# Four RMSNorm factors from two products of ones with the split sum of squares, instead of column factors, a GpSimd root and diagonals

## The chip, the cores and the metric

One core of a Trainium2 chip runs the whole program. The metric is the device time of one execution in microseconds; the kernel before took 1065.73 us, the median of three runs (1065.53 to 1066.01). The core's engines are TensorE (PE in the profile, its weight loads PEld), VectorE (DVE), ScalarE (ACT), GpSimd (POOL) and SyncE (SP), which issues nearly all of the transfers.

## The reference

A trunk of four layers over one sequence of 256 tokens with 1024 channels, all in float32. Each layer adds a token mixer and then a squared-ReLU MLP; each of these begins with an RMSNorm:

```python
def _rmsnorm(x, g):
    return x * lax.rsqrt(jnp.mean(x * x, axis=-1, keepdims=True) + EPS) * g

def _sqrelu_mlp(h, w1, w2):                 # w1: 1024 x 4096, w2: 4096 x 1024
    return jnp.square(jax.nn.relu(h @ w1)) @ w2

for i in range(4):                          # mixers: LRU, SGU, short conv, LRU
    x = x + mixer[i % 3](_rmsnorm(x, norm_mix_g[i]))
    x = x + _sqrelu_mlp(_rmsnorm(x, norm_mlp_g[i]), mlp_w1[i], mlp_w2[i])
return _rmsnorm(x, final_norm_g)
```

The LRU mixer multiplies the normed x by a 1024 x 2560 matrix; half of the result is a GELU branch, the other half goes through a causal convolution over 4 tokens, two gates with 16 blocks of 80 x 80 each, and a linear recurrence over the tokens. The short convolution's first matrix is 1024 x 3072.

## The kernel before

**Layout and numbers.** Channels lie on the 128 partitions and the 256 tokens along the free axis, so x is eight pieces of 128x256, held in pairs (x_105 to x_108). TensorE runs its large products in fp32r, a rounded form of float32, and keeps the accuracy by splitting each operand into a rounded part (hi) and the rest (lo): `mm3` (line 252) makes three products for each tile, hi by hi, hi by lo, lo by hi. Activations are split where they are made. Line 292 (ScalarE) and 293 (VectorE) make `xs`, the split x times the norm's gain; a norm's factor, one number for each token, is multiplied in only behind the first product.

**Weights.** SyncE streams them in chunks of 128x2048 into `raw` buffers. ScalarE rounds each half (line 186, `whi`) and VectorE subtracts (line 189, `wlo`), up to four chunks ahead of the product, into five pairs of buffers. These casts and splits are most of what both engines do.

**The norm's factor.** ScalarE squares x (line 303) and VectorE adds the eight pieces up (lines 308, 309) into `sum`, 128x256: what is left is the sum over the 128 partitions. There are two ways to finish.

`Scales` (six norms: the four mixers', and those of MLP 0 and 3):
- `first_mm` (line 331): two products, in plain float32, with `sum` as the stationary side and two columns of ones as the moving one. Tokens now lie on the partitions, two columns of 128. The trace has four records for these two products.
- `factor`: ScalarE copies 128x2 out of PSUM (line 314); GpSimd takes the reciprocal root by an integer seed (line 315) and three Newton steps (lines 318 to 321), and splits the result (lines 338, 339).
- `diagonals` (line 348): VectorE multiplies the identity by each of the four columns, 128x128 each.
- `second_mm` (line 361): two products of a matrix of ones by the diagonals, 128x256, which lay the factors out as a row on all partitions.
- `copy` (line 365): ScalarE takes that row, `rs`, out of PSUM. VectorE multiplies by it: line 486 in the MLP's hidden tiles, 744 and 824 in the LRU mixers.

`LateScale` (MLP 1 and 2) splits `sum` itself (lines 376, 377) and makes two products of ones by its halves (line 382), which gives the row of sums on all partitions at once; a reciprocal follows (lines 384, 385). The squared ReLU lets it do without the root, and its factor is wanted only behind the whole MLP.

The norm of the last layer's end works in another way; neither it nor the late ones change.

**Order.** TensorE's instructions stand as the program writes them; a helper, `in_mm(4, {k: f})`, runs over k = 0 to 7 (the eight pieces of x), four tiles of `mm3` for each k, and calls f behind step k. On VectorE and ScalarE a list scheduler sets the order by priority, and `SOON` (100) lifts a norm's steps. Two stretches are written out by hand: the first hidden tiles of an MLP by `MLP_STEPS` (C and S are a weight half's cast and split, h0 and h1 the next step of a pair of hidden tiles, `row` the copy of line 365), and each LRU mixer by a string in `LRU_STEPS`, in which P is one step of TensorE's list, `na nv nd nb nr` are `first_mm`, `factor`, `diagonals`, `second_mm` and `copy`, and for the pairs of tiles 0 to 4 `x` is the product with the row (line 744), `K` the convolution's first tap on ScalarE (line 752), `k` its other three taps on VectorE (line 758). Then come the gates (TensorE, lines 702, 710 and 717), their activations on ScalarE (line 770) and the recurrence. Line 803 loads the root's table on ScalarE, line 782 that of the exponential.

In an MLP, `first` (product, root and diagonals) stands behind k = 5 of the first block, `second_mm` behind k = 3 of the next. In the short convolution `first` stands behind k = 6 and `second` behind k = 3 of the following group.

Of the kernel before, what the change touches and what calls it, by code (L numbers as in the profile page):

```python
# [78 lines left out]
)  # L79


# [1 line left out]

HEAD_STEPS = "x0 w x1 w w x2 x3 q0 w w x4 x5 q1 w w x6 x7 q2 w q3"

MLP_STEPS = "C S row C h0 S h0 h0 h0 C h1 S h1 h1 h1 C S"

MLP_STEPS_LATE = "C S C h0 h0 h0 S h0 C h1 h1 h1 S h1 C S"

LATE_SPLIT, LATE_SUM = 3, 4  # L90

UNSPLIT = (0, 1)

# [17 lines left out]
def trunk(ctx: ExitStack, tc: tile.TileContext, xT, consts, sbias, first, weights, out, widths, whole, causal):  # L113
# [26 lines left out]
    def wtile(dtype=F32, name="wk"):  # L140
        return wide.tile([P, 2, T], dtype, name=name, tag="wk", bufs=N_WIDE)
# [182 lines left out]
    class Scales:  # L324
# [42 lines left out]
        def second(self):  # L367
            self.second_mm()
            self.copy()

    class LateScale:


# [17 lines left out]
    def in_mm(nm, hooks={}):  # L391

        banks = [bank() for _ in range((nm + 1) // 2)]
        parts = [(0, KD)] if nm == 2 else [(0, KD // 2), (KD // 2, KD)]
        for k0, k1 in parts:
            w_hi, w_lo = chunk(k1 - k0, nm * P)
            for k in range(k0, k1):
                for m in range(nm):
                    s = slice(m * P, (m + 1) * P)
                    o = banks[m // 2][:, (m % 2) * T:(m % 2 + 1) * T]  # L400
                    mm3(o, w_hi[:, k - k0, s], w_lo[:, k - k0, s], xs_now[k][0], xs_now[k][1],
                        start=k == 0 and m % 2 == 0, stop=k == KD - 1)
                if k in hooks:
                    hooks[k]()
        return [b.rearrange("p (j t) -> p j t", t=T) for b in banks]
# [68 lines left out]
    def mlp(nxt):  # L474


        late = nxt[0] is not None and nxt[1] > KD
        scale = LateScale() if late else Scales()

        def hidden_steps(ps, srcs):  # L480

            u, hi, lo, sq = wtile(name="u"), wtile(F32R, "hi"), wtile(F32R, "lo"), wtile(name="hsq")
            if late:
                yield nc.scalar.activation(u, ps, AF.Relu)  # L484
            else:
                yield nc.vector.scalar_tensor_tensor(out=u, in0=ps, scalar=0.0, in1=both(scale.row), op0=MAX, op1=MULT)  # L486
            yield nc.scalar.activation(hi, u, AF.Square)  # L487
            yield nc.scalar.activation(sq, u, AF.Square)  # L488
            srcs += tiles_of((hi, lo))
            yield nc.vector.tensor_tensor(out=lo, in0=sq, in1=hi.bitcast(F32), op=SUB)  # L490

        def hidden(banks):
            srcs = []
            for ps in banks:
                for _ in hidden_steps(ps, srcs):
                    pass
            return srcs

        def hidden_in_order(banks):

            srcs, pairs, in_order = [], {}, chain()
            for step in (MLP_STEPS_LATE if late else MLP_STEPS).split():
                if step in "CS":
                    in_order((casts if step == "C" else splits).pop(0)())
                elif step == "row":
                    in_order(scale.copy())
                else:
                    i = int(step[1:])
                    if i not in pairs:
                        pairs[i] = hidden_steps(banks[i], srcs)  # L510
                    in_order(next(pairs[i]))
            for steps in pairs.values():
                for _ in steps:
                    raise ValueError("steps of the hidden tiles are left")
            return srcs

        def second(acc, b, srcs):
            if b == NF - 1 and nxt[0] is None:

                x = x_res[KD // 2 - 1][:, 1, :]  # L520
                nc.vector.tensor_tensor(out=x, in0=acc[KD // 2 - 1][:, T:], in1=x, op=ADD)
                apart.append(bank())
                out_mm(acc, srcs, 4 * b, 4 * NF, apart[0])
            elif b == NF - 1:
                out_mm(acc, srcs, 4 * b, 4 * NF)
            else:
                for h in range(2):
                    out_mm(acc, srcs[2 * h:2 * h + 2], 4 * b + 2 * h, 4 * NF)

        apart = []  # L530
        placed[0] = True
        banks = in_mm(4, {} if late else {5: scale.first})
        acc = None
        for b in range(1, NF):
            hooks = {}
            if late and b == LATE_SPLIT:
                scale.split()
            if late and b == LATE_SUM:
                hooks = {3: scale.sum}
            if not late and b == 1:  # L540
                hooks = {3: scale.second_mm}
            nxt_banks = in_mm(4, hooks)
            if acc is None:
                before = hidden_in_order(banks)
                acc = [bank() for _ in range(KD // 2)]
                placed[0] = False
                with tc.high_priority(offset=-LATER):
                    make_parts()
            now = hidden(nxt_banks)
            second(acc, b - 1, before)  # L550
            before = now
        second(acc, NF - 1, before)
        if nxt[0] is None:
            return add_last(acc, apart[0])
        return add_residual(acc, *nxt, scale.row if late else None)
# [36 lines left out]
    class Mixer:  # L592


        def __init__(self, layer):
            self.layer = layer
            self.scale = Scales()
            self.banks = {"branch": [], "gated": [], "gates": {}}
            self.xr, self.xc, self.hs, self.gs, self.parts = {}, {}, {}, {}, {}
            self.rg, self.ig, self.qs, self.t = {}, {}, {}, {}  # L600
            self.acc = None
            self.in_order = chain()
            self.tensor = self.tensor_steps()
# [118 lines left out]
            return self.xc[m // 2][:, m % 2, :]  # L722


        def na(self):
            self.scale.first_mm()

        def nb(self):
            self.scale.second_mm()
# [86 lines left out]
        def z(self, i):  # L816
            self.hs[i] = h = self.rg[i]
            return [nc.vector.tensor_tensor_scan(out=h[:, j, :], data0=self.qs[i][:, j, :], data1=self.ig[i][:, j, :],
                                                 initial=0.0, op0=MULT, op1=ADD) for j in range(2)]


        def g(self, i):
            self.gs[i] = wtile(name="gate")
# [102 lines left out]


    def mixer_c(layer):
        scale = Scales()
        conv = []  # L930
        for b in range(2):
            gc = []
            g_banks = in_mm(4, {} if b else {6: scale.first})
            x_banks = in_mm(4, {} if b else {3: scale.second})
            for ps in g_banks:
                t = wtile(name="gc")
                nc.vector.tensor_tensor(out=t, in0=ps, in1=both(scale.row), op=MULT)
                gc.append(t)
            for i, ps in enumerate(x_banks):
                xv = wtile(name="xv")  # L940
                nc.vector.tensor_tensor(out=xv, in0=ps, in1=both(scale.row), op=MULT)
                nc.vector.tensor_tensor(out=xv, in0=xv, in1=gc[i], op=MULT)
                y = wtile(name="cv")
                for j in range(2):
                    m = 4 * b + 2 * i + j

                    def tap(n):
                        return col("c_conv_w", (layer * 3 + n) * KD + m)

                    nc.scalar.activation(y[:, j, :], xv[:, j, :], AF.Copy, scale=tap(2))  # L950
                    for n in (1, 0):
                        d = 2 - n
                        nc.vector.scalar_tensor_tensor(
                            out=y[:, j, d:], in0=xv[:, j, :T - d], scalar=tap(n), in1=y[:, j, d:],
                            op0=MULT, op1=ADD)
                conv.append(y)
        srcs = []
        for b in range(2):
            for i, ps in enumerate(in_mm(4)):
                y = conv[2 * b + i]  # L960
                gb = wtile(name="gb")
                nc.vector.tensor_tensor(out=gb, in0=ps, in1=both(scale.row), op=MULT)
                nc.vector.tensor_tensor(out=y, in0=y, in1=gb, op=MULT)
                srcs += tiles_of(split(y))
        return out_proj(srcs, 4)
# [230 lines left out]
```

## Time and profile before

| what | us |
|---|---|
| median of three runs | 1065.73 |
| the profiled execution's own time | 1065.78 |
| its span (first to last instruction) | 1064.1 |
| SP's main queue (q1), 201.75 MB | 55.7% of 16 DMA engines over the span |
| GpSimd, root's seed of line 315, 7 instructions | 12.9 |
| VectorE, diagonals of line 348, 24 instructions | 5.4 |

The granted clock of TensorE is 0.999 over the span. A row of the timeline gives the start in us, the busy time of a run of like instructions, engine, line, operation, tiles written and read, shape and how many; in square brackets stands the idle time ahead of it and what ended that. A grouped row gives the count, then the busy time and the mean ns of one, then the idle time ahead of them.

In this execution the norms' first products (line 331) start at 18.27 us in LRU layer 0, 111.26 in MLP 0, 531.75 in the short convolution, 792.50 in LRU layer 1 and 888.49 in MLP 3.

### The profile page before, as it was taken

To read this page: it belongs to the slowest core of one execution; us is meant where nothing else is said; L and a number is where in the kernel's file an instruction comes from. 1 tells how busy PE (TensorE), PEld (TensorE's weight loads), DVE (VectorE), ACT (ScalarE), POOL (GpSimd) and SP (SyncE) were. 2 spreads that over 40 slices of the span, in tenths; PEclk is the share of its full clock that TensorE was granted. 3 is DMA by queue.
4 is the path that set the end of the run, shared out by engine and by line. 5 is a ranking of instruction groups with operands and counts; after the bars stand their busy time and mean duration, and the time that the engine had idled before them with its cause. 6 is when DMAs were issued, how large, how long until landed. Compare 5 with 4: busy or idle time off the path is not lost.

```text
span 1064.1 us, 21687 instructions
## 1 busy us (share of the span) xinstructions
PE 1057.1 (99%) x9138; PEld 1044.4 (98%) x9138; DVE 712.6 (67%) x936; ACT 603.6 (57%) x851; POOL 48.4 (5%) x135
## 2 busy tenths in 40 slices
PE   9999999999999999999999999999999999999997
PEld 9999999999999999999999999999999999999997
DVE  7999765555758754545787765454578997755553
ACT  7697554454574754445544474455555975644442
POOL 2400100000210000000010000000010001000000
PEclk9999999999999999999999999999999999999999
DMA  9656575555556566555466466555545445855401
GB/s 341 252 234 218 173 282 190 195 193 190 190 177 216 178 210 207 188 194 178 157 235 200 159 221 204 193 189 184 194 154 177 179 145 184 294 197 194 138 1 40
DMA packets 58417, 203.39 MB, mean 191 GB/s; under 512 B 6608, under 2 KB 7760, under 8 KB 58320
## 3 DMA queue, kind: packets, MB, share of 16 engines
q1 hardware_dynamic: 58176, 201.75, 55.7%
q8 instruction: 71, 1.16, 0.4%
q14 instruction: 26, 0.21, 0.1%
q10 hardware_dynamic: 144, 0.26, 0.1%
HBM read 200.94 MB, written 1.05 MB: 190 GB/s over the span
## 4 chain that ended last, share of the span: by engine, by line
PE 99%; DVE 0%; DVEq 0%; issue 0%
PE ps L252 91%; PE ps L868 2%; PE ps L702 2%; PE ps L653 1%; PE ps L674 1%; PE ps L710 0%; PE ps L258 0%; PE ps L717 0%; PE ps L904 0%; PE ps L649 0%; PE ps L331 0%; PE ps L361 0%; PE ps L977 0%; PE ps L984 0%; DVE o L1001 0%; DVEq L1192 0%
## 5 line engine op out<-in xcount | busy, mean ns | idle before, releaser
L189 DVE TENSOR_TENSOR wlo<-raw,whi 128x1024 fp32r<-128x1024 f32 (+1 forms) x377 | 440.8, 1201 | 220.9 <-ACT whi L186 220.8
L252 PE MATMUL ps<-xs,whi 128*128 128x256 f32 x3120 | 533.8, 276 | 0.0
L186 ACT CAST whi<-raw 128x1024 fp32r<-128x1024 f32 (+1 forms) x377 | 373.4, 1030 | 274.8 <-issue 160.0
L252 PEld LDWEIGHTS ps<-xs,whi 128*128 128x128 f32 x3120 | 469.8, 188 | 1.3 <-ACT rg L782 0.4
L252 PE MATMUL ps<-xs,wlo 128*128 128x256 f32 x1560 | 430.7, 276 | 0.0
L252 PE MATMUL ps<-hi,whi 128*128 128x256 f32 x1296 | 357.9, 276 | 0.0
L252 PE MATMUL ps<-hi,wlo 128*128 128x256 f32 x1296 | 357.7, 276 | 0.0
L252 PE MATMUL ps<-lo,whi 128*128 128x256 f32 x1296 | 357.7, 276 | 0.0
L252 PEld LDWEIGHTS ps<-xs,wlo 128*128 128x128 f32 x1560 | 292.9, 188 | 0.0
L252 PEld LDWEIGHTS ps<-hi,whi 128*128 128x128 f32 x1296 | 243.3, 188 | 0.0
L252 PEld LDWEIGHTS ps<-lo,whi 128*128 128x128 f32 x1296 | 243.3, 188 | 0.0
L252 PEld LDWEIGHTS ps<-hi,wlo 128*128 128x128 f32 x1296 | 243.3, 188 | 0.0
L490 DVE TENSOR_TENSOR lo<-hsq,hi 128x512 fp32r<-128x512 f32 x64 | 44.0, 688 | 52.3 <-ACT hsq L488 51.3
L292 ACT ACTIVATE xs<-x,cst 128x256 fp32r<-128x256 f32 x64 | 29.1, 501 | 33.7 <-DVE x L438 31.9
L487 ACT ACTIVATE hi<-u 128x512 fp32r<-128x512 f32 x64 | 40.3, 630 | 10.9 <-DVE u L486 10.4
L484 ACT ACTIVATE u<-ps 128x512 f32<-128x512 f32 x32 | 18.9, 592 | 48.2 <-PE ps L252 48.2
L315 POOL TENSOR_SCALAR rc<-rc 128x2 int32<-128x2 int32 x7 | 12.9, 1842 | 685.0 <-ACT rc L314 685.0
L488 ACT ACTIVATE hsq<-u 128x512 f32<-128x512 f32 x64 | 39.5, 617 | 0.0
L486 DVE SCALAR_TENSOR_TENSOR u<-ps,rs 128x512 f32<-128x512 f32 x32 | 22.0, 687 | 20.8 <-PE ps L252 16.3
L293 DVE SCALAR_TENSOR_TENSOR xs<-x,cst,xs 128x256 fp32r<-128x256 f32 x64 | 28.7, 481 | 8.8 <-ACT xs L292 8.8
L758 DVE SCALAR_TENSOR_TENSOR xc<-xr,cst,xc 128x255 f32<-128x255 f32 (+2 forms) x60 | 24.0, 472 | 0.0
L309 DVE TENSOR_TENSOR sum<-sum,sq 128x256 f32<-128x256 f32 x52 | 21.9, 420 | 1.1 <-ACT sq L456 0.6
(137 smaller groups left out, 515.9 us busy)
## 6 DMA issues: line engine op xcount, KB each, us to landing
raw<-weights SPq DMA_DIRECT2D x369, 512.0 KB, 4.2
raw<-first SPq DMA_DIRECT2D x16, 256.0 KB, 4.4
raw<-weights SPq DMA_DIRECT2D x4, 384.0 KB, 6.6
x<-xT SPq DMA_DIRECT2D x8, 128.0 KB, 4.2
out<-o SPq DMA_DIRECT2D x3, 256.0 KB, 2.6
sb<-sbias SPq DMA_DIRECT2D x2, 256.0 KB, 4.1
out<-o ACTq DMA_DIRECT2D x1, 256.0 KB, 2.9
cst<-consts SPq DMA_DIRECT2D x1, 128.0 KB, 5.7
```

What stands on the lines that cost most here:

```text
L186: return nc.scalar.copy(out=hi[:, s], in_=raw[:, e])
L189: return nc.vector.tensor_tensor(out=lo[:, s], in0=raw[:, e], in1=hi.bitcast(F32)[:, s], op=SUB)
L252: nc.tensor.matmul(ps, a, b, start=start and n == 0, stop=stop and n == 2, skip_group_check=True)
L292: return (nc.scalar.activation(xs[:, hi], x, AF.Copy, scale=g), nc.vector.scalar_tensor_tensor(out=xs[:, lo], in0=x, scalar=g, in1=xs.bitc ...
L293: nc.vector.scalar_tensor_tensor(out=xs[:, lo], in0=x, scalar=g, in1=xs.bitcast(F32)[:, hi], op0=MULT, op1=SUB))
L309: return [nc.vector.tensor_tensor(out=sq_now[0], in0=sq_now[0], in1=sq[:, j, :], op=ADD) for j in range(2)]
L486: yield nc.vector.scalar_tensor_tensor(out=u, in0=ps, scalar=0.0, in1=both(scale.row), op0=MAX, op1=MULT)
L487: yield nc.scalar.activation(hi, u, AF.Square)
L488: yield nc.scalar.activation(sq, u, AF.Square)
L490: yield nc.vector.tensor_tensor(out=lo, in0=sq, in1=hi.bitcast(F32), op=SUB)
L702: nc.tensor.matmul(banks[m][:, e, :], block(), self.tile_of(m), start=e == 0, stop=False, skip_group_check=True)
L758: return [nc.vector.scalar_tensor_tensor(out=c[:, j, d:], in0=x[:, j, :T - d], scalar=self.tap(3 - d, 2 * i + j), in1=c[:, j, d:], op0=MUL ...
```

## The change

A third class, `RowScale`, takes the place of `Scales` in four norms: MLP 0 and 3, the short convolution, and LRU layer 1 (`ROW_LAYERS = (1,)`). LRU layer 0 and the SGU mixer keep `Scales`. It splits the sum as `LateScale` does, makes the same two products of ones, and then works on the whole row, 128x256, on every partition: ScalarE takes the root (a function that needs a table of its own) and a copy out of PSUM, VectorE a reciprocal and one Newton step.

```diff
+    class RowScale:
+        def split(self):
+            self.parts = wtile(F32R, "sums")
+            return [nc.scalar.copy(out=self.parts[:, 0, :], in_=sq_now[0]),
+                    nc.vector.tensor_tensor(out=self.parts[:, 1, :], in0=sq_now[0],
+                                            in1=self.parts.bitcast(F32)[:, 0, :], op=SUB)]
+        def split_soon(self):
+            with tc.high_priority(offset=SOON):
+                self.split()
+        def sum(self):
+            self.ps = bank()[:, :T]
+            for j in range(2):
+                nc.tensor.matmul(self.ps, ones_r, self.parts[:, j, :], start=j == 0, stop=j == 1)
+        def factor(self):
+            pair = wtile(name="vt")
+            v, t = pair[:, 0, :], pair[:, 1, :]
+            y = self.row = work.tile([P, T], F32, name="rs", tag="rs", bufs=2)
+            return [nc.scalar.activation(t, self.ps, AF.Sqrt, scale=1.0 / D, bias=eps),
+                    nc.scalar.activation(v, self.ps, AF.Copy, scale=1.0 / D, bias=EPS),
+                    nc.vector.reciprocal(out=y, in_=t),
+                    nc.vector.scalar_tensor_tensor(out=t, in0=y, scalar=-0.5, in1=y, op0=MULT, op1=MULT),
+                    nc.vector.tensor_tensor(out=t, in0=t, in1=v, op=MULT),
+                    nc.vector.scalar_tensor_tensor(out=y, in0=t, scalar=1.5, in1=y, op0=ADD, op1=MULT)]
+        def first(self):
+            self.sum()
+            with tc.high_priority(offset=SOON):
+                self.factor()
...
-MLP_STEPS = "C S row C h0 S h0 h0 h0 C h1 S h1 h1 h1 C S"
+MLP_STEPS = "C S C h0 S h0 h0 h0 C h1 S h1 h1 h1 C S"
...
-        scale = LateScale() if late else Scales()
+        scale = LateScale() if late else RowScale()
...
-        banks = in_mm(4, {} if late else {5: scale.first})
+        if not late:
+            scale.split_soon()
+        banks = in_mm(4, {} if late else {6: scale.first})
...
-            if not late and b == 1:
-                hooks = {3: scale.second_mm}
...
-            self.scale = Scales()
+            self.scale = RowScale() if layer in ROW_LAYERS else Scales()
...
+        def ns(self):
+            with tc.high_priority(offset=SOON):
+                return self.scale.split()
         def na(self):
-            self.scale.first_mm()
+            (self.scale.sum if self.layer in ROW_LAYERS else self.scale.first_mm)()
...
+        def wE(self):
+            t = work.tile([P, 1], F32, name="warm", tag="warm")
+            return nc.scalar.activation(t, ones[:, :1], AF.Exp)
...
-        scale = Scales()
+        scale = RowScale()
+        scale.split_soon()
...
-            g_banks = in_mm(4, {} if b else {6: scale.first})
-            x_banks = in_mm(4, {} if b else {3: scale.second})
+            g_banks = in_mm(4, {} if b else {7: scale.first})
+            x_banks = in_mm(4)
```

The string of LRU layer 1 is rewritten up to its first gates. Its steps `nd`, `nb` and `nr` are gone, `ns` (the split of the sum) is new, the `x`, `K` and `k` steps stand earlier, some weight splits later, and `wE` is a tiny exponential ahead of the gates, so that its table is loaded there. What this moves shows best in the engines' own order. Line numbers of the changed program are shifted by its new lines (252 is now 254, 189 is 191, 186 is 188, 309 is 311, 303 is 305, 744 is 782, 752 is 790, 758 is 796, 486 is 522, 490 is 526).

VectorE in MLP 0, from the last addition to the norm's sum to the first hidden tile, before:

```order
L309 TENSOR_TENSOR sum<-sum,sq 128x256
L189 TENSOR_TENSOR wlo<-raw,whi 128x1024 x3
L348 TENSOR_SCALAR diag<-eye,rc_1571 128x128 x2
L348 TENSOR_SCALAR diag<-eye,rc_1572 128x128 x2
L486 SCALAR_TENSOR_TENSOR u<-ps,rs 128x512
```

and now (`sums` is the split sum, `vt` the root and the copy, `rs` the row):

```order
L311 TENSOR_TENSOR sum<-sum,sq 128x256
L191 TENSOR_TENSOR wlo<-raw,whi 128x1024
L379 TENSOR_TENSOR sums<-sum,sums 128x256
L191 TENSOR_TENSOR wlo<-raw,whi 128x1024 x2
L397 RECIPROCAL rs<-vt 128x256
L398 SCALAR_TENSOR_TENSOR vt<-rs 128x256
L399 TENSOR_TENSOR vt<-vt 128x256
L400 SCALAR_TENSOR_TENSOR rs<-vt,rs 128x256
L522 SCALAR_TENSOR_TENSOR u<-ps,rs 128x512
```

One weight split now stands ahead of the sum's own split, and the other two ahead of the reciprocal; the same three splits stood ahead of the diagonals.

VectorE in LRU layer 1, from the last addition to the sum to the convolution's first pair, before:

```order
L309 TENSOR_TENSOR sum<-sum,sq 128x256
L189 TENSOR_TENSOR wlo<-raw,whi 128x1024 x5
L348 TENSOR_SCALAR diag<-eye,rc_9710 128x128 x2
L348 TENSOR_SCALAR diag<-eye,rc_9711 128x128 x2
L189 TENSOR_TENSOR wlo<-raw,whi 128x1024 x2
L744 TENSOR_TENSOR xr<-ps,rs 128x512 x3
L189 TENSOR_TENSOR wlo<-raw,whi 128x1024
L758 SCALAR_TENSOR_TENSOR xc<-xr,cst,xc 128x255 x2
L758 SCALAR_TENSOR_TENSOR xc<-xr,cst,xc 128x254 x2
L758 SCALAR_TENSOR_TENSOR xc<-xr,cst,xc 128x253 x2
```

and now:

```order
L311 TENSOR_TENSOR sum<-sum,sq 128x256
L379 TENSOR_TENSOR sums<-sum,sums 128x256
L191 TENSOR_TENSOR wlo<-raw,whi 128x1024 x2
L397 RECIPROCAL rs<-vt 128x256
L398 SCALAR_TENSOR_TENSOR vt<-rs 128x256
L399 TENSOR_TENSOR vt<-vt 128x256
L400 SCALAR_TENSOR_TENSOR rs<-vt,rs 128x256
L191 TENSOR_TENSOR wlo<-raw,whi 128x1024 x2
L782 TENSOR_TENSOR xr<-ps,rs 128x512 x2
L191 TENSOR_TENSOR wlo<-raw,whi 128x1024
L796 SCALAR_TENSOR_TENSOR xc<-xr,cst,xc 128x255 x2
L796 SCALAR_TENSOR_TENSOR xc<-xr,cst,xc 128x254 x2
```

Between the sum and the convolution's first pair stood eight weight splits; five are left there, and the others now stand among the pairs.

ScalarE beside it, from the last square to the convolution's taps, before:

```order
L303 ACTIVATE sq<-x_108 128x512
L186 CAST whi<-raw 128x1024 x3
L314 ACTIVATE rc<-ps 128x2
L186 CAST whi<-raw 128x1024 x4
L365 COPY rs<-ps 128x256
L186 CAST whi<-raw 128x1024
L752 ACTIVATE xc<-xr,cst 128x256 x6
L186 CAST whi<-raw 128x1024 x2
```

and now:

```order
L305 ACTIVATE sq<-x_108 128x512
L188 CAST whi<-raw 128x1024 x2
L378 CAST sums<-sum 128x256
L188 CAST whi<-raw 128x1024
L395 ACTIVATE vt<-ps,eps 128x256
L396 ACTIVATE vt<-ps 128x256
L188 CAST whi<-raw 128x1024
L790 ACTIVATE xc<-xr,cst 128x256 x4
L188 CAST whi<-raw 128x1024 x3
L790 ACTIVATE xc<-xr,cst 128x256 x2
L188 CAST whi<-raw 128x1024
L862 ACT_TABLE_LOAD
```

Eight casts stood between the last square and the first taps; four are left there, and the others now stand among and behind the taps. The table of the exponential is loaded behind the sixth tap. None is loaded for the root here: the one that the short convolution's root loads is still in.

More of the change, by code (lines that the diff above doesn't have):

```diff
@@ L72 @@
     "P S P S P",
[6 rows of a table removed]
[6 rows of a table added]
 )
 HEAD_STEPS = "x0 w x1 w w x2 x3 q0 w w x4 x5 q1 w w x6 x7 q2 w q3"
-MLP_STEPS = "C S row C h0 S h0 h0 h0 C h1 S h1 h1 h1 C S"
+MLP_STEPS = "C S C h0 S h0 h0 h0 C h1 S h1 h1 h1 C S"
 MLP_STEPS_LATE = "C S C h0 h0 h0 S h0 C h1 h1 h1 S h1 C S"
 LATE_SPLIT, LATE_SUM = 3, 4
+ROW_LAYERS = (1,)
 UNSPLIT = (0, 1)
@@ L504, in hidden_in_order @@
                     in_order((casts if step == "C" else splits).pop(0)())
-                elif step == "row":
-                    in_order(scale.copy())
                 else:
```

12 rows, old and new, of the table LRU_STEPS are left out of this document.

## The prediction

> **What bounds the kernel now.** I read the page first, then TensorE's waits, then its timeline at the lines the change touches, then the other engines beside them.
>
> ```profile
> span 1064.1 us, 21687 instructions
> PE 1057.1 (99%) x9138; PEld 1044.4 (98%) x9138; DVE 712.6 (67%) x936; ACT 603.6 (57%) x851; POOL 48.4 (5%) x135
> ...
> PE 99%; DVE 0%; DVEq 0%; issue 0%
> ```
>
> TensorE is busy from end to end and the chain that ended last is TensorE. Its list of waits has one row in all:
>
> ```profile
> PE ps L258 <- DVE ones L263: 1.1, 1, 1.1
> ```
>
> So time can only come from products taken out of its stream, from stalls too short for that list, or be lost to a new wait. A busy share hides short stalls, because the matmuls overlap; I measure from start to start. In MLP 0, around the first product of a norm (line 331):
>
> ```profile
> 111.14 0.28 PE L252 MATMUL ps<-xs,wlo 128*128 128x256 f32 x1
> 111.26 0.50 PE L331 MATMUL ps<-ones,sum 128*128 128x2 f32 x4
> ...
> 111.94 0.28 PE L252 MATMUL ps<-xs,wlo 128*128 128x256 f32 x1
> ...
> 112.28 0.28 PE L252 MATMUL ps<-xs,wlo 128*128 128x256 f32 x1
> ```
>
> From one wlo product to the next lie three matmuls. Undisturbed that is 112.28 - 111.94 = 0.34 us; across line 331 it is 0.80, so these narrow products cost 0.46. The second product (line 361, two matmuls) there:
>
> ```profile
> 119.76 0.28 PE L252 MATMUL ps<-xs,wlo 128*128 128x256 f32 x1
> 119.88 0.40 PE L361 MATMUL ps<-diag,ones_r 128*128 128x256 f32 x2
> ...
> 120.35 0.28 PE L252 MATMUL ps<-xs,wlo 128*128 128x256 f32 x1
> ```
>
> 0.59 - 0.34 = 0.25 us. In LRU layer 1 it is another matter:
>
> ```profile
> 801.00 0.28 PE L252 MATMUL ps<-xs,wlo 128*128 128x256 f32 x1
> 801.32 0.69 PE L361 MATMUL ps<-diag,ones_r 128*128 128x256 f32 x2
> ...
> 802.08 0.28 PE L252 MATMUL ps<-xs,wlo 128*128 128x256 f32 x1
> ```
>
> 1.08 - 0.34 = 0.74: the same two matmuls, and a stall of 0.49. Its cause stands on GpSimd and VectorE:
>
> ```profile
> 793.30 2.68 POOL L315 TENSOR_SCALAR rc<-rc 128x2 int32<-128x2 int32 x1 [255.60 <-ACT rc L314]
> ...
> 800.44 0.18 POOL L338 CAST rc<-rc 128x2 fp32r<-128x2 f32 x1
> ```
>
> ```profile
> 800.65 0.91 DVE L348 TENSOR_SCALAR diag<-eye,rc 128x128 fp32r<-128x128 f32 x4 [2.54 <-POOL rc L338]
> ```
>
> GpSimd's root takes from 793.30 to 800.62, VectorE waits 2.54 for it, and the diagonals end at 801.56, past the turn of the product at about 801.1. The grouped rows say that no other place is like this:
>
> ```profile
> L331 PE MATMUL ps<-ones,sum 128*128 128x2 f32 x24 | 3.0, 230 | 0.0
> L361 PE MATMUL ps<-diag,ones_r 128*128 128x256 f32 x12 | 2.7, 294 | 0.0
> ```
>
> Six norms, 6 x 0.50 = 3.0 and 5 x 0.40 + 0.69 = 2.7.
>
> **Part by part: TensorE.** Of these six norms four change. Each loses its line 331 and its line 361 and gets two matmuls of ones by the split sum. Exactly these two already run in the late norms of MLP 1 and 2 (line 382):
>
> ```profile
> 429.36 0.28 PE L252 MATMUL ps<-xs,wlo 128*128 128x256 f32 x1
> 429.48 0.40 PE L382 MATMUL ps<-sums,ones_r 128*128 128x256 f32 x2
> ...
> 430.31 0.28 PE L252 MATMUL ps<-xs,wlo 128*128 128x256 f32 x1
> ```
>
> Here 0.95 covers two spacings of 0.34, so the pair costs 0.27. Three norms: 0.46 + 0.25 - 0.27 = 0.44 each, 1.32. LRU layer 1: 0.46 + 0.74 - 0.27 = 0.93. **Sum 2.25 us.** The new place of the product is not in this trace; its price lies between two plain matmuls (2 x 0.34 / 3 = 0.23) and the narrow ones (0.46); I take 0.27, the same instruction. At 0.23 the gain is 2.41, at 0.46 it is 1.49.
>
> **The other engines.** Per norm GpSimd loses 15 small operations, VectorE four diagonals, ScalarE a 128x2 and a 128x256 copy. New durations:
>
> ```profile
> L293 DVE SCALAR_TENSOR_TENSOR xs<-x,cst,xs 128x256 fp32r<-128x256 f32 x64 | 28.7, 481 | 8.8 <-ACT xs L292 8.8
> L309 DVE TENSOR_TENSOR sum<-sum,sq 128x256 f32<-128x256 f32 x52 | 21.9, 420 | 1.1 <-ACT sq L456 0.6
> L385 DVE RECIPROCAL rs<-rs 128x256 f32<-128x256 f32 x2 | 3.5, 1746 | 0.0
> ```
>
> ```profile
> L803 ACT ACT_TABLE_LOAD x4 | 5.1, 1283 | 0.1
> L384 ACT ACTIVATE rs<-ps 128x256 f32<-128x256 f32 x2 | 0.7, 373 | 0.0
> ```
>
> VectorE gets 0.42 + 1.75 + 0.48 + 0.42 + 0.48 = 3.55 and loses 0.91: 2.6 more per norm, about 2.3 where neighbours overlap. ScalarE gets three operations of 128x256. The root is unmeasured at this shape; I take the 0.37 of line 384, which also leaves PSUM at that shape, for all three, and even twice that would leave the idle time below uncrowded. There are three more table loads in all (root in MLP 0 and the short conv, GELU again in mixer B; in LRU layer 1 one only moves forward, by wE). I cost all of this at nothing, because of what covers it:
>
> ```profile
> 111.80 0.17 ACT L314 ACTIVATE rc<-ps 128x2 f32<-128x2 f32 x1 [2.95 <-PE ps L331]
> 120.31 0.37 ACT L365 COPY rs<-ps 128x256 f32<-128x256 f32 x1 [8.34 <-PE ps L361]
> ```
>
> ```profile
> 110.17 0.42 DVE L309 TENSOR_TENSOR sum<-sum,sq 128x256 f32<-128x256 f32 x1
> 110.51 3.49 DVE L189 TENSOR_TENSOR wlo<-raw,whi 128x1024 fp32r<-128x1024 f32 x3
> ```
>
> In MLP 0 ScalarE stands idle for 2.95 and 8.34 us where the load and the root go. The product moves one k step (4 x 0.34 = 1.36) behind 111.26, to 112.62. Its second half waits for VectorE: the sum ends at 110.59, one weight split (1.14 apart in the row of three) stands ahead, then 0.42: about 112.07, 0.55 ahead of its turn. From there root, reciprocal behind two more splits and three short operations give the row at about 117.3, where the copy now ends at 120.68: hidden tiles come earlier, not later. MLP 3 has the same order; the short conv's product stands a k step later still.
>
> The trace has 1.28 us per table load, and ScalarE's next activation follows it at once. The Trainium skill, "ScalarE: Activation LUTs", section "What ACT_TABLE_LOAD costs", speaks against a change that adds switches: about 2.66 us each, drain included. No row here shows that drain; by it three more switches would be 8.0 instead of 3.9 us of ScalarE, an estimate.
>
> **LRU layer 1 is where the cover is thinnest**, so I work it out in the clock of this trace (every engine starts the stage shifted alike).
>
> ```profile
> 790.96 0.42 DVE L309 TENSOR_TENSOR sum<-sum,sq 128x256 f32<-128x256 f32 x1
> ...
> 803.76 1.87 DVE L744 TENSOR_TENSOR xr<-ps,rs 128x512 f32<-128x512 f32 x3
> ...
> 806.68 7.17 DVE L758 SCALAR_TENSOR_TENSOR xc<-xr,cst,xc 128x255 f32<-128x255 f32 x18
> ```
>
> ```profile
> 802.20 0.36 ACT L365 COPY rs<-ps 128x256 f32<-128x256 f32 x1
> ...
> 804.47 3.07 ACT L752 ACTIVATE xc<-xr,cst 128x256 f32<-128x256 f32 x6 [0.95 <-DVE xr L744]
> ```
>
> ```profile
> 812.74 4.48 PE L702 MATMUL ps<-xc,raw 128*128 128x256 f32 x20
> ```
>
> ```profile
> L702 PE MATMUL ps<-xc,raw 128*128 128x256 f32 x80 | 18.0, 380 | 0.0
> ```
>
> The sum ends at 791.4, its halves at 792.2; the product runs at 793.9; the root starts about 0.6 later (111.26 to 111.80 is that distance above, 0.54) and ends at 794.9, reciprocal to 796.7, row at 797.9 instead of 802.56. VectorE then does two splits (800.2) and two xr (801.4), and waits for ScalarE, which does four conv products (to 802.9) and a weight cast (803.9). Then split, first conv pair (six at 0.40), split, xr, second pair, split, third pair: 805.0, 807.4, 808.5, 809.2, 811.5, 812.7, and the operation that the fifth gate tile needs ends at 814.7. The gates' twenty records, the last 0.38 long, start (4.48 - 0.38) / 19 = 0.216 apart, four to a tile, so that tile starts at 812.74 + 16 x 0.216 = 816.2, less the 0.93 that TensorE gains here: 815.3. **0.55 us to spare**, against 816.2 - 813.5 = 2.7 now (the row of eighteen ends at 813.85, the fifth of the last six one spacing earlier). No wait, but near.
>
> **The rivals.**
> 1. *The 0.49 stall belongs to this one execution.* GpSimd's first operation there took 2.68, and the mean of its seven is 1.84:
>
> ```profile
> L315 POOL TENSOR_SCALAR rc<-rc 128x2 int32<-128x2 int32 x7 | 12.9, 1842 | 685.0 <-ACT rc L314 685.0
> ```
>
> Then the gain is 1.76: 1064.0. Against it: runs from 1065.53 to 1066.01 leave room for only part of it.
> 2. *The split sum is late.* If one more weight split slips ahead of it in the MLPs, 1.14 - 0.55 = 0.59 of wait in MLP 0 and, by the same order, in MLP 3, 1.2 in all: 1064.7. For it: 0.55 is little. Against it: the queue's order is fixed and shows one split.
> 3. *Table loads end up on the path.* Three loads at 1.28 are 3.9: 1067.4. Against it: the idle 2.95 and 8.34 of ScalarE. By the price in "What ACT_TABLE_LOAD costs" of the Trainium skill's "ScalarE: Activation LUTs" it would be about 1071.5, an estimate.
> The fourth rival needs the stage's row of busy times (stretch, its length, then PE, PEld, DVE, ACT, POOL, the clock and the DMA share):
>
> ```profile
> 803.00:821.00 18.00, 18.00 (x155) 16.26 (x154) 18.00 (x39) 10.21 (x20) 0.00 (x0) 1.00 0.45 148
> ```
>
> 4. *Slower: the third conv pair is late at the gates of LRU layer 1.* If the 2.5 us that VectorE waits for ScalarE's cast (801.4 to 803.9) come again ahead of the second and the third pair, the pair is 5.0 late, TensorE stands 5.0 - 0.55 = 4.45: 1068.0. It decides from 2.25 + 0.55 = 2.8 us of lateness on. For it: VectorE is busy without a gap here already. Against it: ScalarE's queue has the next two casts right behind the first.
>
> 5. *It does not do what it says*: the freed 2.25 us are taken back at a later wait of the kind that rows now hide: 1065.7. Against it: no such wait is in the list.
>
> **How the numbers follow.** The profiled execution took 1065.78 us (span 1064.1 and 1.7 around it), 0.05 over the median of 1065.73. 1065.78 - 2.25 = 1063.53, against the median 1063.48: **1063.5**. Chances: forecast 0.74 (1063.1 to 1063.9, the prices of the product and the spread of the runs), rival 1 0.09, rival 2 0.08, rival 3 0.03, rival 4 0.04, rival 5 0.02. The range 1063.1 to 1064.2 takes in the forecast and rival 1, 0.83. About 0.2% is what a measurement of this kernel can tell from no change; that is 2.13 us here, so the line is 1063.60, just above the forecast. Two thirds of the forecast's chance lie below it: faster 0.50; slower is rival 4, 0.04; the rest, 0.46, within.
>
> **What would show it.** Right: TensorE's spacing across the new product is 0.25 to 0.30 over 0.34 in all four norms, no gap near the old 801, VectorE's diagonals only in LRU layer 0 and mixer B, no new row in TensorE's waits. Wrong: the second ones product starts late behind VectorE's subtraction in MLP 0; the gate products of LRU layer 1 start late behind the third conv pair; a spacing above 0.46 over plain.

## The result, and the profile after

The changed kernel takes **1063.76 us** (median of 18 runs, 1063.40 to 1064.14), the kernel before in the same runs 1065.61 (1065.14 to 1066.20): 1.85 us less. The ratio is 0.9982, 95% interval 0.9976 to 0.9989. Forecast were 1063.5 us (1063.1 to 1064.2) and a gain of 2.25. The profiled execution took 1063.91.

The head of the page, after:

```profile
span 1062.2 us, 21602 instructions
PE 1055.3 (99%) x9122; PEld 1042.7 (98%) x9122; DVE 722.1 (68%) x940; ACT 610.3 (57%) x859; POOL 27.9 (3%) x75
```

VectorE is busy for 9.5 us more, ScalarE for 6.7 more, GpSimd for 20.5 less; the span is 1.9 shorter. TensorE's list of waits still has the one row of the start:

```profile
PE ps L260 <- DVE ones L265: 1.1, 1, 1.1
```

TensorE's timeline at the new product (line 389), in MLP 0 and then in LRU layer 1, and the stretch of LRU layer 1 in which it stood before:

```profile
112.88 0.28 PE L254 MATMUL ps<-xs,wlo 128*128 128x256 f32 x1
113.00 0.40 PE L389 MATMUL ps<-sums,ones_r 128*128 128x256 f32 x2
...
113.48 0.28 PE L254 MATMUL ps<-xs,wlo 128*128 128x256 f32 x1
```

```profile
793.24 0.28 PE L254 MATMUL ps<-xs,wlo 128*128 128x256 f32 x1
793.36 0.40 PE L389 MATMUL ps<-sums,ones_r 128*128 128x256 f32 x2
...
793.84 0.28 PE L254 MATMUL ps<-xs,wlo 128*128 128x256 f32 x1
...
801.00 0.28 PE L254 MATMUL ps<-xs,wlo 128*128 128x256 f32 x1
801.11 0.39 PE L254 MATMUL ps<-xs,whi 128*128 128x256 f32 x2
801.34 0.28 PE L254 MATMUL ps<-xs,wlo 128*128 128x256 f32 x1
```

0.60 from wlo to wlo in both, 0.26 over the plain 0.34; over ten matmuls, which takes in the small lengthening of the neighbours, it is 0.27 at all four places. Where the stall of 0.49 was, the spacing is the plain 0.34.

What stands beside it, VectorE and ScalarE in MLP 0:

```profile
112.00 0.41 DVE L379 TENSOR_TENSOR sums<-sum,sums 128x256 fp32r<-128x256 f32 x1
...
114.61 1.74 DVE L397 RECIPROCAL rs<-vt 128x256 f32<-128x256 f32 x1
...
117.37 0.42 DVE L400 SCALAR_TENSOR_TENSOR rs<-vt,rs 128x256 f32<-128x256 f32 x1
```

```profile
111.40 1.28 ACT L395 ACT_TABLE_LOAD   x1
113.44 0.47 ACT L395 ACTIVATE vt<-ps,eps 128x256 f32<-128x256 f32 x1 [0.76 <-PE ps L389]
```

The table load lies in idle time, with 0.76 left behind it; the row is ready at 117.79, the old copy ended at 120.68. And LRU layer 1, VectorE and then TensorE's gates:

```profile
797.08 0.42 DVE L400 SCALAR_TENSOR_TENSOR rs<-vt,rs 128x256 f32<-128x256 f32 x1
...
803.47 1.22 DVE L191 TENSOR_TENSOR wlo<-raw,whi 128x1024 fp32r<-128x1024 f32 x1 [2.49 <-ACT whi L188]
...
812.21 2.45 DVE L796 SCALAR_TENSOR_TENSOR xc<-xr,cst,xc 128x255 f32<-128x255 f32 x6
```

```profile
811.31 4.48 PE L736 MATMUL ps<-xc,raw 128*128 128x256 f32 x20
```

The operation that the fifth gate tile needs ends one spacing of 0.40 before 814.66, at 814.26; the tile's turn is 811.31 + 16 x 0.216 = 814.77. That is 0.51 to spare, forecast 0.55.

**Where the missing 0.4 is.** Both traces have the product by diagonals of LRU layer 0 (line 361, now 363), to which nothing changes in any engine's order. Before, after, and two later traces of before and after (e9, e11):

```profile
29.69 0.39 PE L361 MATMUL ps<-diag,ones_r 128*128 128x256 f32 x2
```

```profile
30.07 0.40 PE L363 MATMUL ps<-diag,ones_r 128*128 128x256 f32 x2
```

```profile
29.07 0.40 PE L361 MATMUL ps<-diag,ones_r 128*128 128x256 f32 x2
```

```profile
29.79 0.40 PE L363 MATMUL ps<-diag,ones_r 128*128 128x256 f32 x2
```

It starts 0.38 later after than before, and between two executions of one kernel it moves by 0.62 (before) and 0.28 (after). From there to the end of the span it is 1064.07 - 29.69 = 1034.38 before and 1062.20 - 30.07 = 1032.13 after: 2.25 less. The experiments below are read by this split.

### The profile page after: what moved, and what is told of

The parts are those of the page before. It is cut to its first block, busy times and chain, and to the rows that moved or that the text cites. A ratio compares the mean times of both kernels' runs of the same rounds, so it can differ in the third digit from the quotient of the medians.

```text
span 1062.2 us, 21602 instructions
## 1 busy us (share of the span) xinstructions
PE 1055.3 (99%) x9122; PEld 1042.7 (98%) x9122; DVE 722.1 (68%) x940; ACT 610.3 (57%) x859; POOL 27.9 (3%) x75
## 3 DMA queue, kind: packets, MB, share of 16 engines
HBM read 200.94 MB, written 1.05 MB: 190 GB/s over the span
## 4 chain that ended last, share of the span: by engine, by line
PE 99%; DVE 0%; DVEq 0%; issue 0%
PE ps L254 92%; PE ps L910 2%; PE ps L736 2%; PE ps L687 1%; PE ps L708 1%; PE ps L744 0%; PE ps L260 0%; PE ps L751 0%; PE ps L946 0%; PE ps L683 0%; PE ps L1020 0%; PE ps L1027 0%; PE ps L389 0%; DVE o L1044 0%; PE ps L333 0%; DVEq L1235 0%
## 5 line engine op out<-in xcount | busy, mean ns | idle before, releaser
L910 PE MATMUL ps<-whi,xs 128*128 128x512 f32 x64 | 20.5, 394 | 0.0
```

The lines of the kernel that those rows point to most:

```text
L910: nc.tensor.matmul(ps[c], xs[a][:, s], b[:, k, :], start=kk == 0 and n == 0, stop=kk == KD - 1 and n == 2)
```

## The experiments

Kernels e1 to e4 ran together, e5 to e8 together, each with 11 runs beside 33 of the kernel before (medians 1065.66 and 1065.74); e9 to e11 are one execution each. For each trace, the start of the product by diagonals of LRU layer 0 and the rest of the span from there, and the difference of the medians:

| kernel | start | rest | rest, less before | median, less before |
|---|---|---|---|---|
| before | 29.69 | 1034.38 | | |
| before, e9 | 29.07 | 1034.39 | | |
| before, e10 | 29.25 | 1034.38 | | |
| after | 30.07 | 1032.13 | -2.25 | -1.85 |
| after, e11 | 29.79 | 1032.14 | -2.24 | |
| e1, LRU layer 1 alone | 29.74 | 1033.46 | -0.92 | -0.64 |
| e2, all but LRU layer 1 | 29.55 | 1032.83 | -1.55 | -1.15 |
| e3, before, diagonals' product later | 29.34 | 1033.88 | -0.50 | -0.30 |
| e4, MLP products earlier | 29.72 | 1033.75 | -0.63 | -0.35 |
| e5, one more reciprocal | 30.18 | 1033.62 | -0.76 | -0.65 |
| e6, more table loads | 29.99 | 1032.15 | -2.23 | -2.17 |
| e8, one product | 29.86 | 1031.68 | -2.70 | -2.57 |

e7 has no such product in LRU layer 0 and is read by itself. The 95% intervals of these medians are 1.4 to 1.9 us wide, and those of e1, e3, e4 and e5 take in no change at all; so the parts rest on the traces, one for each of e1 to e8, and traces of one kernel agree in the rest of the span within 0.01.

**e1, e2: one part at a time.** e1 keeps `RowScale` in LRU layer 1 only; e2 everywhere but there, with the old string of steps:

```diff
...
-        scale = LateScale() if late else RowScale()
+        scale = LateScale() if late else Scales()
...
```

```diff
...
-ROW_LAYERS = (1,)
+ROW_LAYERS = ()
...
```

> The new factors in LRU layer 1 alone; MLP 0 and 3 and the short convolution keep the column factors and the diagonals. Theory (the gain is a sum of prices on TensorE's stream, 0.93 of it from this norm): 0.93 us under the kernel before; in the trace the spacing over plain is 0.46 and 0.25 at the first and second product of MLP 0, the short convolution and MLP 3, 0.27 at the one product of LRU layer 1, and no 0.49 of stall. Rival A (what medians show is 1.85 and not 2.25, so one of the two parts gives about 0.4 less): only 0.5 under. Rival B (the stall was of one execution): 0.44 under.

> The new factors in MLP 0 and 3 and the short convolution; LRU layer 1 keeps the old norm and the old order of steps. Theory: 3 x 0.44 = 1.32 us under the kernel before, and the trace shows the old stall again around the product by diagonals of LRU layer 1, 0.74 over plain in place of 0.25. Rival A (the missing 0.4 is here): 0.9 under. Rival B (the stall was of one execution): 0.25 there, and 1.8 under.

In e1's trace the rest of the span is 0.92 shorter, 0.93 was expected. In e2 it is 1.55 and not 1.32, and the cause is the old stall, TensorE in LRU layer 1 of e2:

```profile
799.98 0.28 PE L254 MATMUL ps<-xs,wlo 128*128 128x256 f32 x1
800.10 0.65 PE L363 MATMUL ps<-diag,ones_r 128*128 128x256 f32 x2
...
800.82 0.28 PE L254 MATMUL ps<-xs,wlo 128*128 128x256 f32 x1
```

0.84 - 0.34 = 0.50 over plain, so 0.25 of stall in place of 0.49. Why it is half shows on GpSimd and VectorE there, in the kernel before and then in e2:

```profile
796.89 1.28 POOL L321 TENSOR_TENSOR rc<-rc 128x2 f32<-128x2 f32 x1
796.89 1.22 DVE L189 TENSOR_TENSOR wlo<-raw,whi 128x1024 fp32r<-128x1024 f32 x1 [0.97 <-ACT whi L186]
```

```profile
796.13 1.05 POOL L320 TENSOR_TENSOR rc<-rc 128x2 f32<-128x2 f32 x1
795.87 1.26 DVE L191 TENSOR_TENSOR wlo<-raw,whi 128x1024 fp32r<-128x1024 f32 x1 [0.97 <-ACT whi L188]
```

The long GpSimd operation ends 0.05 to 0.06 behind the end of VectorE's weight split in both; its neighbours take 0.20. In the kernel before it is the fifth of the root, which starts together with the split. In e2 the fifth starts at 795.86, 0.01 ahead of the split, takes 0.20, and only the sixth is caught. So one step less is left when the split ends, and the diagonals come 0.23 earlier against the first product. e3 has the same order as e2.

Rival B (the stall belongs to one execution) was not out yet; rival A (the missing 0.4 in one of the two parts) is: both traces have their prices, and both medians fall short.

**e3: the stall alone.** The kernel before, its second product one step later:

```diff
-    "... nd P S nb C P nr S C P x0 ..."
+    "... nd P S C P nb nr S C P x0 ..."
```

> The kernel before, with the product by diagonals of LRU layer 1 one step of TensorE (four tiles, 1.36 us) later and nothing else. Theory (TensorE waited there for GpSimd's root and the diagonals, which end 0.5 behind its turn): the diagonals are ready 0.9 ahead of the new turn, the spacing falls from 0.74 to 0.25, 0.49 us under the kernel before; VectorE's products with the row do not start later, since VectorE is busy until then. Rival (the stall only moves: the row comes about 0.9 later, and the convolution and the gates with it): the same time as before, with a gap of TensorE at the first gates.

TensorE at the new place of the product, in e3:

```profile
802.01 0.28 PE L252 MATMUL ps<-xs,wlo 128*128 128x256 f32 x1
802.13 0.39 PE L361 MATMUL ps<-diag,ones_r 128*128 128x256 f32 x2
...
802.60 0.28 PE L252 MATMUL ps<-xs,wlo 128*128 128x256 f32 x1
```

0.59, as in the other norms, and 0.50 less in the rest of the span: in this trace moving one instruction is worth what the theory said, and nothing comes back later.

**e4: how much cover the split sum has.** The product of MLP 0 and 3 one k step earlier:

```diff
-        banks = in_mm(4, {} if late else {6: scale.first})
+        banks = in_mm(4, {} if late else {5: scale.first})
```

> The changed kernel with the product of MLP 0 and 3 behind k = 5, where the old product stood, in place of k = 6: 1.36 us earlier. Theory (the subtraction of the sum ends 0.71 and 0.78 ahead of the second product's turn in the changed kernel's trace, about 0.06 goes for the release): TensorE waits 1.36 - 0.65 = 0.71 in MLP 0 and 1.36 - 0.72 = 0.64 in MLP 3, together 1.35 us over the changed kernel. By the estimate of the prediction (0.55 to spare) it would be 1.6. Rival (TensorE's queue hides a wait under one microsecond behind its own matmuls): nothing over the changed kernel.

The rest of the span is 1.62 over the changed kernel's. TensorE and VectorE in MLP 0 of e4:

```profile
111.29 0.28 PE L389 MATMUL ps<-sums,ones_r 128*128 128x256 f32 x1
112.17 0.39 PE L389 MATMUL ps<-sums,ones_r 128*128 128x256 f32 x1 [0.59 <-DVE sums L379]
112.39 0.39 PE L254 MATMUL ps<-xs,whi 128*128 128x256 f32 x2
```

```profile
111.70 0.41 DVE L379 TENSOR_TENSOR sums<-sum,sums 128x256 fp32r<-128x256 f32 x1
```

The second product starts 0.06 behind the subtraction's end and 0.88 behind the first (undisturbed 0.12): 0.76. The matmul behind it follows after 0.22 in place of 0.12, so this wait costs 0.85 in all, and the same count in MLP 3 gives 0.75. The rival (the queue hides it) is out. My 1.35 left out this lengthening. The list of waits shows 0.59: it counts from the end of the busy time and so hides about a third of what the wait costs.

**e5: how near LRU layer 1 is to a wait.** One more reciprocal ahead of the row, in LRU layer 1 only:

```diff
...
+                    *([nc.vector.reciprocal(out=wtile(name="rx")[:, 0, :], in_=t)] if self.twice else []),
                     nc.vector.reciprocal(out=y, in_=t),
...
             self.scale = RowScale() if layer in ROW_LAYERS else Scales()
+            self.scale.twice = True
...
```

> The changed kernel with one more reciprocal of 128x256 (1.75 us, into a tile that nobody reads) on VectorE ahead of the row of LRU layer 1. Theory (the third conv pair is what the gates wait for next, with 0.5 to spare, and VectorE's idle 2.5 us is no cover, because ScalarE's taps and casts behind the row come later by as much): the fifth gate tile waits 1.78 - 0.5 = 1.25, and the kernel is 1.25 us over the changed one. Rival A (VectorE's idle 2.5 takes it up): no change. Rival B (more is late behind it, the gates of the second group and the recurrence): over 1.8.

VectorE and TensorE in e5:

```profile
805.18 1.23 DVE L191 TENSOR_TENSOR wlo<-raw,whi 128x1024 fp32r<-128x1024 f32 x1 [2.49 <-ACT whi L188]
...
813.93 2.44 DVE L800 SCALAR_TENSOR_TENSOR xc<-xr,cst,xc 128x255 f32<-128x255 f32 x6
```

```profile
811.42 3.61 PE L740 MATMUL ps<-xc,raw 128*128 128x256 f32 x16
816.23 1.10 PE L740 MATMUL ps<-xc,raw 128*128 128x256 f32 x4 [1.20 <-DVE xc L800]
```

The wait is at the fifth gate tile. VectorE's idle 2.49 is there again, unshortened: it only moved, since ScalarE's taps and casts wait for the same row. So rival A falls, and rival B (over 1.8) with the rest of the span. The tile starts at 816.23 in place of 811.42 + 16 x 0.216 = 814.88: 1.35, and with longer spacings behind it 1.48 in the rest of the span. The pair starts 813.93 - 812.21 = 1.72 later than in the changed kernel, 0.11 of it because the stage does (its product at 793.47 for 793.36): 1.61, of which 1.61 - 1.35 = 0.26 was to spare and not 0.51. The pair's fifth operation ends at 815.97, and another 0.26 pass before TensorE goes on; these are the difference.

**e6: more table loads.** An exponential of one column behind the sum's rounding in MLP 0 and 3 and the short convolution. The trace has 20 loads in place of 16: six for these three norms, where the changed kernel has two (about three were expected): in MLP 3 the table is already in.

```diff
                 self.split()
+                t = work.tile([P, 1], F32, name="warm", tag="warm")
+                nc.scalar.activation(t, self.parts.bitcast(F32)[:, 0, :1], AF.Exp, scale=1e-6)
```

> The changed kernel with a one-column exponential behind the sum's rounding in MLP 0 and 3 and the short convolution, so that each of the three norms loads two tables more or less back to back (the exponential's, then the root's); six loads of 1.28 us in place of about three. Theory (ScalarE's idle time ahead of the root and ahead of the hidden tiles covers them): the time of the changed kernel within 0.2 us; the next activation starts within 0.1 us of a load's end. Rival (loads end up on the path): 1.28 x 3 = 3.8 over. By the Trainium skill (ScalarE: Activation LUTs, What ACT_TABLE_LOAD costs) a drain of 1.38 us would stand behind each load, which the rows would show as idle time.

The rest of the span is that of the changed kernel within 0.02. ScalarE in MLP 0 of e6:

```profile
111.39 1.28 ACT L386 ACT_TABLE_LOAD   x1
112.68 0.20 ACT L386 ACTIVATE warm<-sums 128x1 f32<-128x1 f32 x1
112.91 1.28 ACT L397 ACT_TABLE_LOAD   x1
114.20 0.47 ACT L397 ACTIVATE vt<-ps,eps 128x256 f32<-128x256 f32 x1
```

111.39 + 1.28 = 112.67, and the next activation starts at 112.68. The root is 0.76 later than in the changed kernel, and the reciprocal starts at 114.71 in place of 114.61. In MLP 3, where three loads now stand in a row, it starts 1.6 later (891.51 for 889.95). TensorE waits in neither. The drain of about 1.38 us that the Trainium skill adds to a load (ScalarE: Activation LUTs, What ACT_TABLE_LOAD costs) is not in these rows: 0.01 lies behind each load, 0.02 ahead of it.

**e7: the same in LRU layer 0.** `RowScale` there too, its product behind step 13 of TensorE's list:

```diff
-ROW_LAYERS = (1,)
+ROW_LAYERS = (0, 1)
...
-    "P9 na P nv P2 C P S C P S C P S C nd P C S P C S nb P S nr x0 ..."
+    "P9 ns P3 C P S na nv C P S C P S C P C S P C S P S x0 ..."
```

> The changed kernel with the new factors in LRU layer 0 as well: the product behind step 13 of TensorE's list, root and reciprocal where GpSimd's root and the diagonals were. Theory: 0.48 + 0.25 - 0.27 = 0.46 us under the changed kernel, with no wait of TensorE in the first 40 us. Rival (VectorE is busy for 97% of the time from 18 to 31 us here, and gets 2.6 us more; ScalarE gets two more table loads): weight splits come late and TensorE stands for 1 to 3 us, slower than the changed kernel.

1066.54 us, 2.8 over the changed kernel, where 0.46 under it was expected. TensorE has no wait from 10 to 40 us; its waits stand some 45 us behind the new operations, at the first product of the output matrix:

```profile
73.58 0.28 PE L254 MATMUL ps<-xs,wlo 128*128 128x256 f32 x1
74.51 0.38 PE L254 MATMUL ps<-hi,whi 128*128 128x256 f32 x1 [0.66 <-ACT hi L878]
76.37 0.38 PE L254 MATMUL ps<-lo,whi 128*128 128x256 f32 x1 [1.48 <-DVE lo L883]
```

and the windows of e7 there (the stretch, its length, busy time of PE, PEld, DVE, ACT, POOL, then TensorE's clock, the DMA share and GB/s):

```profile
74.50:76.00 1.50, 0.38 (x1) 0.19 (x1) 1.47 (x3) 1.50 (x4) 0.00 (x0) 1.00 0.00 0
76.00:77.00 1.00, 0.63 (x5) 0.63 (x6) 1.00 (x3) 1.00 (x3) 0.00 (x0) 1.00 0.00 0
77.00:79.00 2.00, 2.00 (x13) 2.00 (x13) 2.00 (x5) 1.98 (x4) 0.00 (x0) 0.61 0.00 0
79.00:81.00 2.00, 2.00 (x12) 2.00 (x12) 2.00 (x5) 1.99 (x3) 0.00 (x0) 0.53 0.00 0
```

VectorE is busy for all of the 28 us from 32 to 60, as it already is in the changed kernel, so its added work is not absorbed; it comes out where TensorE next needs a result of the recurrence. VectorE's step for the second wait (line 883) starts at 75.63, in the changed kernel at 73.20. ScalarE's two more table loads are not the cause: ahead of its cast for the first wait (line 878) it stands idle for 2.57, waiting for VectorE.

The two waits cost 0.93 + 1.86 less two spacings of 0.11: 2.57. Behind them the granted clock falls. The 48 spacings from 73.58 to 83.38 take 4.36 more than at 0.113 each, so 1.79 is left: 1.61 of it in the 3.5 us at the slower clock (77.43 to 80.96), the rest in slightly longer spacings beside them. The profiled execution is one of the slower ones (1067.20; the eleven run from 1066.13 to 1067.70), and 4.36 - 0.46 = 3.9 is more than the 2.8 of the medians. How much of this an average execution loses, and whether its clock falls, is not shown. The rival was right in its sign and wrong in its place: no wait of TensorE is for a weight split.

**e8: one product.** The lower part of the sum is left out, and the subtraction that makes it:

```diff
...
-            for j in range(2):
-                nc.tensor.matmul(self.ps, ones_r, self.parts[:, j, :], start=j == 0, stop=j == 1)
+            nc.tensor.matmul(self.ps, ones_r, self.parts[:, 0, :], start=True, stop=True)
```

> The changed kernel with one product of ones by the rounded sum in place of two in its four norms; the rest of the sum (its lower part) is left out, and the subtraction with it. Theory: a product is worth one spacing, 0.113, so the site costs 0.16 over plain in place of 0.27, and the four norms save 0.45 us. Rival (a site's cost is that of changing the stationary operand to ones and back, not the number of products): no change in the spacing.

The rest of the span is 0.45 under the changed kernel's, 0.16 over plain at each place. So the rival (no change in the spacing) falls. A product of this kind costs its spacing of 0.113; the other 0.05 is what it does to its neighbours. It has the shortest rest of the span of these kernels, at the price of a rounded sum.

**e9 to e11: the two kernels again.**

> The kernel before once more, for its trace. The medians so far show some 0.25 us less than the sum of prices in each kernel that touches LRU layer 1's norm. Theory (the stall ahead of its product by diagonals is usually about 0.25, and 0.49 only in the execution first profiled, where GpSimd's root took 7.3 us and not 7.1 as in the two other traces that have it): the spacing over plain there is about 0.5, GpSimd from its first to its last step 7.1. Rival (the stall is 0.49 each time, and the rest is lost in the first 30 us): 0.74 again.

> The same once more. Theory: about 0.5 over plain, GpSimd's root 7.1. Rival: 0.74 and 7.3.

> The changed kernel once more, for its trace. Theory (from the product by diagonals of LRU layer 0 on, its stream is fixed): 1032.1 us from the start of that product to the end of the span, as in its first trace (1062.2 - 30.1), while the start itself moves by some tenths from execution to execution. Rival: the later part varies by as much as the start.

My theory fell. TensorE in e9:

```profile
800.38 0.28 PE L252 MATMUL ps<-xs,wlo 128*128 128x256 f32 x1
800.69 0.69 PE L361 MATMUL ps<-diag,ones_r 128*128 128x256 f32 x2
...
801.46 0.28 PE L252 MATMUL ps<-xs,wlo 128*128 128x256 f32 x1
```

1.08, the same 0.74 over plain, in e10 too: three traces of the kernel before have the same stall, and GpSimd's fifth step of 1.28 us where e2 and e3 have a sixth of 1.05; GpSimd from its first to its last step takes 7.3. From LRU layer 0 on, three traces of before agree within 0.01 us, two of after likewise. What varies is the start, by 0.6.

## Why the prediction was right

- **The prices on TensorE** held to the hundredth: 0.46 and 0.25 gone in three norms, 0.46 and 0.74 in LRU layer 1, 0.27 come in four times; 2.25 forecast, 2.25 measured from LRU layer 0 on. e1, e2 and e3 show it by parts, and that the stall is one of them.
- **The cover held.** Forecast in MLP 0: subtraction done at 112.07, row at 117.3; measured 112.41 and 117.79 with a start 0.36 to 0.38 later. In LRU layer 1 0.55 to spare were forecast to the end of VectorE's operation, 0.51 measured; e5 shows that only 0.26 of it can be used, since 0.26 pass between that end and TensorE's start. So the margin that rival 4 counted on was too large, though nothing used it up. The root took 0.47 where 0.37 was assumed, and nothing waited for it.
- **Rival 1** (the stall belongs to one execution): three traces of the same kernel have it alike. But e2 has half of it at the same place with the same string: a start of one GpSimd operation 0.01 earlier or later decides between 0.49 and 0.25, so the size is not fixed. The forecast took the whole 0.49 and was right in the three traces; an execution with half of it would have gained 0.25 less.
- **Rival 2** (the split sum is late) is what e4 makes: its price of 0.59 for each MLP would have been about 0.1 more, for the restart. **Rival 3** falls with e6. **Rival 5** falls: from LRU layer 0 on, the whole 2.25 is gained, and nothing is taken back.
- **What the sum left out** is the start. Forecast was 1063.5, measured 1063.76, and the chances, set just at the bound, leaned on the wrong side of it: 1.85 us is 0.17%, within 0.2%. The forecast also started from 1065.73, and the kernel before came out at 1065.61 beside the changed one; by luck this hides 0.12 of the missing 0.40. The sum took the first 30 us of the profiled execution as they were; they came out 0.38 longer in the trace after. The first 30 us began their last common product at 29.07 to 29.69 in three traces of before and one of e3, and at 29.55 to 30.18 in the eight of the others.
- **What moves the start** stands ahead of everything that the change touches. Of the 0.38 between the two profiled executions, 0.33 lies in the first eight matmuls on x (the last section has them). In five other traces (e2, e3, e4, e6, e9) the list of waits shows TensorE waiting 0.2 to 0.5 at line 331 (now 333) of LRU layer 0 for the sum, whose last addition starts anywhere from 17.14 us (e9) to 18.18 (e5); up to 8 us ScalarE and VectorE wait for the first transfers of x and of the weights.
- **What stays open.** The medians of all eight kernels fall 0.06 to 0.40 (0.23 in the mean) short of the difference in the rest of the span. Each shortfall lies within its interval (for the changed kernel 1.2 to 2.6 us, around 2.25), but all are on one side. Whether that is chance, or the new programs make the start slower although the order of their instructions there is the same, was not settled.

## What to carry to other kernels

Where one engine is busy from end to end, price a change by start-to-start spacings of that engine, site by site; a stall too short for the list of waits shows there, and the sum holds to hundredths. Free time beside it is worth nothing or everything: the same 2.6 us of VectorE work cost nothing in four norms, and in a fifth (e7) the kernel lost 2.8 us, where VectorE was full until the next result that TensorE wanted, 45 us later. An idle gap of an engine is no cover when what ends it waits for the same thing.

## What the runs showed of the hardware

- **The first matmuls run at half pace, for a time that differs between executions.** The first float32 products on x are recorded 0.427 us apart and later 0.22. Before: 2.42 us for eight; after: 2.75:

```profile
5.10 2.42 PE L649 MATMUL ps<-xg,raw 128*128 128x256 f32 x8
```

```profile
5.10 2.75 PE L683 MATMUL ps<-xg,raw 128*128 128x256 f32 x8
```

  Between none and four of these spacings are slow in the thirteen traces; the step to full pace comes 2.9 us (e6, e9) to 5.7 us (after) behind the first matmul at 1.10, while the clock column shows 1.00 throughout. The Trainium skill (TensorE: Matmul & The Clock Gate, "What's actually happening") has half rate until about 3.4 us of activity in a free-running window, and says that the count of cold matmuls changes from run to run. The traces agree that the count changes, and their 2.9 to 5.7 us lie around that figure.
- **Two waits of 0.82 and 1.75 us, one matmul apart, were followed by half the clock** for some 3.5 us (e7: 0.213 us a matmul from 77.6 to 80.8), which cost 1.61 on top of 2.57. The same section has the clock fall after an idle window of about 3.4 us; in this trace it fell behind less idle time than that, with a matmul in it. Behind the single wait of 1.35 in e5 the clock column stays at 1.00.
- **A small GpSimd operation beside a weight split on VectorE is held until the split ends.** Eleven operations of 128x2 in the trace before take over 1 us where most take about 0.2, and ten of them end 0.05 behind the end of a 128x1024 subtraction.
- **A wait costs more than its length:** the first matmul behind it took about 0.1 longer to follow (0.22 for 0.12 in e4).
